# A two-layer encoder trunk: weight sums formed by adding transfers, seven products in the gate half of the second FFN, and the first output group moved forward

## The chip, the core and the metric

The kernel runs on one core of one Trainium2 chip. The time is the device time of one execution in microseconds, taken as the median of several executions. Before the change it was 1288.16 us, the median of three runs (1286.86 to 1289.29).

## The reference, cut to what matters

The trunk has two layers over 512 tokens of 1024 features. A layer mixes tokens (HGRN2 and stick-breaking heads in layer 0, an mLSTM in layer 1) and then runs a causal convolution FFN with a gate. The change is in the two FFNs ("the first network" and "the second network" below), each with an input projection of 1024 to 2 x 2816 and an output projection of 2816 to 1024.

```python
def conv_glu_ffn(h, w_in, conv_w, conv_b, w_out):
    u = jnp.matmul(h, w_in)
    a, g = jnp.split(u, 2, axis=-1)
    a = causal_dwconv(a, conv_w, conv_b)
    return jnp.matmul(jax.nn.gelu(a) * g, w_out)

x = x + g_f * conv_glu_ffn(modulate(x, norm_ffn_g, sh_f, sc_f), ffn_w_in, ffn_conv_w, ffn_conv_b, ffn_w_out)
```

The modulation vectors (`sh_f`, `g_f` and others) come from `c` through `ada_w`: 96 columns, each one transfer of 512 KB and one multiply-and-reduce on VectorE.

## The kernel before, in words

Everything is float32. Features lie on the 128 partitions, tokens along the row. Every operand of a large product is split into a high part (a cast to fp32r on ScalarE, L222) and a low part (the difference on VectorE, L223), and every product is three matmuls: high x high, high x low, low x high. `split_w` does this for weights, `split_act` for activations.

**An FFN (`ffn`, L1130).** The 22 column tiles of 128 of the `a` half and of the gate half are taken in pairs. Pairs 0 and 2 (the opening, the loop over `f0`) are computed directly. The nine pairs from 4 to 20 are "sets". In a set, the `a` half (2 tiles, 1024 x 256 weights against 1024 x 512 activations) is computed by the seven products of Strassen's scheme in its Winograd form (`Seven`): the weight is a 2 x 2 matrix of blocks (128 columns by 512 rows, 256 KB each), the activations too (512 features by 256 tokens). One product (X1 to X7, `Seven.run`) is 12 matmuls of 256 columns. The gate half is computed directly: Y0 and Y1 are 24 matmuls of 512 columns each (`second`).

The sums that the scheme needs are formed on VectorE. On the weight side, `Seven.fetch` loads the four blocks in two transfers, `Seven.prep` forms four sums into the `sums` tiles (L1083, L1084, L1087, L1088) and splits them. On the activation side, `tokens_side(kk)` forms and splits four sums for each of four feature tiles, once per FFN; two are formed after each tile of the second opening pair. `Seven.run` reads the partial results from the PSUM banks (copies `pp`, `u2` on ScalarE, additions into `v` on VectorE, L1113 to L1128). At the end of a set, `post` does the convolution (`act_a`), the activation, the gate and the split (`act_g`), and calls `take(2)`: two ada columns (only the first network has any left; `side`).

**The job list.** The products and gate tiles of a set are jobs, in `ORDER` (`FIRST` in set 4). Output projections (`out_jobs`) are jobs too: one per 256 output columns, with an x update (L385) per 128. Output columns are accumulated in groups of input tiles: six tiles, then four, four, four, and the last four by `halves_out` behind the list. Groups 0, 1 and 2 stand in the sets 6, 10 and 14 behind their third job, group 3 behind the last set. The loop at the end of `ffn` runs nine jobs ahead with the loads of the blocks (`FETCH`) and six ahead with the splits (`LEAD`). A planner orders the instructions of each engine from this program order by its own cost estimates, and places the semaphore waits.

**Queues and buffers.** All transfers are issued by SyncE, in order; one waits there until the buffer it writes is free. `raw` has four buffers of 4 KB per partition (weights as loaded), `sums` two, `ada` two, `ws` ten (split weights), `wq` two of half the size; `work` has 45 tiles for activations. PSUM has four banks `acc` and four `mx`. GpSimd issues no transfer and has small operations outside the FFNs.

## Time and profile before

| | |
|---|---|
| median of three runs | 1288.16 us |
| the profiled execution | 1288.47 us |
| its span | 1286.7 us |
| granted TensorE clock, mean | 0.995 |
| the first FFN, sets and output | about 351 to 645 us |
| the second FFN, sets and output | about 964 to 1253 us |

The page gives busy times for the whole span, then costly groups of instructions. Views of the trace give stretches of time, waits and single instructions. A group's line holds the line of the kernel, the engine, the operation, "out<-in" by tile names, the shape and the count, then busy time and the mean duration of one. TensorE's matmuls overlap, so what one costs is read from start to start.

### The profile page before, as it was taken

To read this page: it belongs to the slowest core of one execution; us is meant where nothing else is said; L and a number is where in the kernel's file an instruction comes from. 1 tells how busy PE (TensorE), PEld (TensorE's weight loads), DVE (VectorE), ACT (ScalarE), POOL (GpSimd) and SP (SyncE) were. 2 spreads that over 40 slices of the span, in tenths; PEclk is the share of its full clock that TensorE was granted. 3 is DMA by queue.
4 is the path that set the end of the run, shared out by engine and by line. 5 is a ranking of instruction groups with operands and counts; after the bars stand their busy time and mean duration, and the time that the engine had idled before them with its cause. 6 is when DMAs were issued, how large, how long until landed. Compare 5 with 4: busy or idle time off the path is not lost.

```text
span 1286.7 us, 18103 instructions
## 1 busy us (share of the span) xinstructions
PE 1246.4 (97%) x6942; PEld 1060.2 (82%) x6942; DVE 917.6 (71%) x1503; ACT 578.9 (45%) x1011; POOL 113.7 (9%) x199
## 2 busy tenths in 40 slices
PE   5999999999989999999999999999999999999997
PEld 4876788899878888888897777778988888888887
DVE  7845788857876776768776869776797475657665
ACT  4454323235452434344446674774455152525432
POOL 0021254400000000000000120221000000000000
PEclk9999999999999999999999999999999999999999
DMA  8823655422434343435423338522232332323211
GB/s 319 296 70 99 220 171 178 135 83 67 147 99 148 120 141 118 140 119 181 136 80 115 98 100 267 157 66 67 66 115 75 106 114 83 112 85 111 86 49 66
DMA packets 47078, 161.04 MB, mean 125 GB/s; under 512 B 5136, under 2 KB 7568, under 8 KB 46992
## 3 DMA queue, kind: packets, MB, share of 16 engines
q1 hardware_dynamic: 46992, 159.89, 38.8%
q8 instruction: 54, 0.88, 0.3%
q14 instruction: 32, 0.26, 0.1%
HBM read 157.77 MB, written 2.10 MB: 124 GB/s over the span
## 4 chain that ended last, share of the span: by engine, by line
PE 86%; DVE 5%; issue 3%; ACT 3%; DMA 2%; POOL 1%; SPq 0%; POOLq 0%; DVEq 0%; ACTq 0%
PE acc L255 13%; PE acc L256 13%; PE acc L257 13%; PE mx L255 5%; PE mx L256 5%; PE mx L257 5%; PE acc L1107 4%; PE acc L1108 4%; PE acc L1109 4%; PE acc L657 2%; PE mx L488 2%; PE mx L659 2%; PE acc L289 1%; PE acc L291 1%; PE acc L290 1%
## 5 line engine op out<-in xcount | busy, mean ns | idle before, releaser
L255 PE MATMUL acc<-hh,wg 128*128 128x512 f32 (+1 forms) x384 | 144.0, 376 | 1.2 <-DVE cv L1148 1.2
L256 PE MATMUL acc<-hl,wg 128*128 128x512 f32 (+1 forms) x384 | 144.4, 376 | 0.0
L257 PE MATMUL acc<-hh,wg 128*128 128x512 f32 (+1 forms) x384 | 144.1, 376 | 0.0
L169 DVE CUSTOM_DVE_ANT_0 adaraw<-adaraw,csb,par 128x1024 f32<-128x1024 f32 x96 | 123.0, 1293 | 4.3 <-DMA adaraw<-adaT 4.2
L256 PE MATMUL mx<-actl,wd 128*128 128x512 f32 x288 | 113.5, 394 | 0.0
L255 PE MATMUL mx<-acth,wd 128*128 128x512 f32 x288 | 112.8, 395 | 0.0
L257 PE MATMUL mx<-acth,wd 128*128 128x512 f32 x288 | 112.1, 394 | 0.0
L255 PE MATMUL acc<-hh,w 128*128 128x512 f32 x256 | 105.6, 412 | 0.0
L222 ACT CAST w<-wraw 128x1024 fp32r<-128x1024 f32 x68 | 71.2, 1051 | 68.5 <-PE acc L256 35.0
L257 PE MATMUL acc<-hh,w 128*128 128x512 f32 x256 | 101.9, 398 | 0.0
L256 PE MATMUL acc<-hl,w 128*128 128x512 f32 x256 | 101.7, 397 | 0.0
L223 DVE TENSOR_TENSOR w<-wraw,w 128x1024 fp32r<-128x1024 f32 x68 | 83.5, 1234 | 24.3 <-ACT w L222 14.6
L1107 PE MATMUL acc<-th,wa 128*128 128x256 f32 x288 | 83.3, 289 | 4.9 <-ACT th L1187 3.5
L222 ACT CAST wg<-wgraw 128x1024 fp32r<-128x1024 f32 x44 | 46.1, 1048 | 86.5 <-PE acc L1108 64.6
L385 DVE SCALAR_TENSOR_TENSOR x<-mx,mod,x 128x512 f32<-128x512 f32 x64 | 47.8, 749 | 52.1 <-PE mx L257 51.7
L255 PEld LDWEIGHTS acc<-hh,wg 128*128 128x128 f32 x384 | 72.1, 188 | 14.8 <-ACT wa L222 1.4
L257 PEld LDWEIGHTS acc<-hh,wg 128*128 128x128 f32 x384 | 72.0, 188 | 13.7 <-DVE wg L223 0.4
L1108 PE MATMUL acc<-tl,wa 128*128 128x256 f32 x288 | 81.7, 284 | 1.1 <-DVE tl L1188 1.1
L256 PEld LDWEIGHTS acc<-hl,wg 128*128 128x128 f32 x384 | 72.1, 188 | 12.3
L1109 PE MATMUL acc<-th,wa 128*128 128x256 f32 x288 | 81.4, 283 | 0.0
L336 POOL TENSOR_TENSOR nr<-nv,mhalf 128x2 f32<-128x2 f32 (+1 forms) x9 | 7.7, 854 | 815.4 <-ACT nv L334 815.4
L222 ACT CAST wa<-was 128x1024 fp32r<-128x1024 f32 x36 | 37.8, 1050 | 69.1 <-PE mx L256 29.8
(307 smaller groups left out, 3254.9 us busy)
## 6 DMA issues: line engine op xcount, KB each, us to landing
adaraw<-adaT SPq DMA_DIRECT2D x96, 512.0 KB, 4.4
wraw<-wflat SPq DMA_DIRECT2D x76, 512.0 KB, 4.2
waraw<-wflat SPq DMA_DIRECT2D x44, 512.0 KB, 3.7
wgraw<-wflat SPq DMA_DIRECT2D x44, 512.0 KB, 4.4
wdraw<-wflat SPq DMA_DIRECT2D x32, 512.0 KB, 3.8
x<-xT SPq DMA_DIRECT2D x8, 256.0 KB, 4.6
wdraw<-wflat SPq DMA_DIRECT2D x8, 256.0 KB, 2.7
outT<-fin SPq DMA_DIRECT2D x6, 256.0 KB, 2.4
```

Of the source, the lines that this page charges most:

```text
L169: return nc.vector.tensor_tensor_reduce(out=tile_, in0=tile_, in1=csb, scale=1.0, scalar=pc("ada_b", o), op0=ALU.mult, op1=ALU.add, accum_ ...
L222: nc.scalar.copy(hi, src)
L223: nc.vector.tensor_sub(lo, src, hi.bitcast(F32))
L255: nc.tensor.matmul(out, ah, bh, start=start, stop=False)
L256: nc.tensor.matmul(out, ah, bl, start=False, stop=False)
L257: nc.tensor.matmul(out, al, bh, start=False, stop=stop)
L385: nc.vector.scalar_tensor_tensor(x[j][:, sl], ps, g, x[j][:, sl], op0=ALU.mult, op1=ALU.add)
L488: nc.tensor.matmul(lps[:, c * 64:(c + 1) * 64].rearrange("p (b m) -> p b m", m=m), k[:, s], qu, start=True, stop=True)
L657: nc.tensor.matmul(vps[i], act[:, i * P:(i + 1) * P], wt_[:, 0:512], start=s0, stop=s1)
L1107: nc.tensor.matmul(ps, hi[:, ks], bh, start=first and kk == 0, stop=False, skip_group_check=True)
L1108: nc.tensor.matmul(ps, hi[:, ks], bl, start=False, stop=False, skip_group_check=True)
L1109: nc.tensor.matmul(ps, lo[:, ks], bh, start=False, stop=kk == 3, skip_group_check=True)
```

## The change

The weight sums are no longer formed on VectorE. The blocks of a half lie one after the other in HBM, and a sum is formed by loading one block pair into a tile and adding others onto it with transfers that accumulate (`accum_op`), which GpSimd issues. A seven-product half now takes seven tile pieces: for products 1 and 2 a plain load of two blocks; for 5 and 7 a load and one addition of two blocks; for 3 and 6 a load, two additions of two blocks and one of one block; for 4 a load of one. Each of the four steps is issued three jobs (`STAGE`) after the one before, the last three jobs before `LEAD` (5). The signs are taken over by the token side and by the evacuations (a factor -1 in an instruction that was there).

In the second network (`PAIRS`) the gate half goes through seven products as well, so a set there has 14 jobs (`TWO`). The output groups are four, four, four, four, two and four tiles, and stand in the sets 4, 8, 12 and 16, behind the third job (fourth in `TWO`); the group of two, with 512 columns per job, stands behind the last set. All token sums are formed at the first job instead of within the opening. The ada columns come one with each half of an output job (of 128 columns) of the groups after the first. `raw` now has two buffers inside the lists; two more each for the tiles `pr` and `qw`, and two halves `rawq`. Outside the lists weights take turns in `raw`, `pr` and `qw`. `work` has 44 tiles.

```diff
-    NW, NR, NS, NQ, NX, NA = 45, 4, 10, 2, 2, 2
+    NW, NR, NS, NQ, NA = 44, 2, 10, 2, 2
...
+    def load_blocks(tile_, at, i0, n, add=False):
+        o, m = at + i0 * P * T, n * P * T
+        eng = nc.gpsimd if add else nc.sync
+        eng.dma_start(tile_.rearrange("p (b c) -> p b c", b=n),
+                      wflat[o:o + m].rearrange("(b p c) -> p b c", b=n, p=P),
+                      **({"accum_op": ALU.add} if add else {}))
...
+    homes = ("raw", "pr", "qw")
+    turn = [0, 3]
+    def raw_tile(name, n=D, tag=None):
+        if n <= T:
+            return rawp.tile([P, T], F32, tag="rawq", name=nm(name), bufs=NQ)[:, :n]
+        if tag is None:
+            tag = homes[turn[0] % turn[1]]
+            turn[0] += 1
+        return rawp.tile([P, D], F32, tag=tag, name=nm(name))[:, :n]
...
-    ORDER = ("X1", "X5", "X6", "X2", "X7", "Y0", "X3", "X4", "Y1")
-    FIRST = ("Y0", "X1", "Y1", "X5", "X6", "X2", "X7", "X3", "X4")
-    PREPS = ("X1", "X5", "Y0", "X7", "X4")
-    OUT_AT, LEAD, FETCH = 3, 6, 9
+    ONE = ("X1", "X5", "X6", "X2", "X7", "Y0", "X3", "X4", "Y1")
+    ONE_FIRST = ("X1", "X2", "Y0", "X5", "X6", "Y1", "X7", "X3", "X4")
+    TWO = ("X1", "Y1", "X2", "Y2", "X5", "Y5", "X6", "Y6", "X3", "X7", "Y7", "Y3", "X4", "Y4")
+    LEAD, STAGE = 5, 3
+    PAIRS = (False, True)
...
+        def stages(self):
...
+            return {
+                1: [lambda: start(1, 0, 2)],
+                5: [lambda: add(5, 2), lambda: start(5, 1, 2)],
+                6: [lambda: load_blocks(t[6][:, 0:T], self.at, 3, 1, True), lambda: add(6, 2), lambda: add(6, 1),
+                    lambda: start(6, 0, 2)],
+                4: [lambda: start(4, 3, 1)],
+            }
         def prep(self, n):
-            (a11, a12), (a21, a22) = ((r[:, 0:T], r[:, T:D]) for r in self.raw)
...
-                nc.vector.tensor_add(src[:, 0:T], a21, a22)
-                nc.vector.tensor_sub(self.s2, src[:, 0:T], a11)
...
+            hi, lo = split_w(self.t[n], self.name)
+            for i, m in enumerate({1: (2, 1), 5: (7, 5), 6: (3, 6), 4: (4,)}[n]):
                 self.pieces[m] = hi[:, i * T:(i + 1) * T], lo[:, i * T:(i + 1) * T]
...
-        groups = ((0, 6), (6, 4), (10, 4), (14, 4), (18, 4))
+        groups = ((0, 4), (4, 4), (8, 4), (12, 4), (16, 2), (18, 4))
...
-                    tokens_side(2 * s)
-                    tokens_side(2 * s + 1)
-            take(2)
...
         def out_jobs(gi):
             f0, fn = groups[gi]
-            for cb in range(4):
+            cols = 1024 // fn
+            for cb in range(D // cols):
...
+                        if gi > 0:
+                            take(1)
...
+        def seven_at(sev, n, j):
+            for i, f in enumerate(sev.stages_of[n]):
+                fetches.append((j - LEAD - (i + 1) * STAGE, len(fetches), f))
+            return lambda: sev.prep(n)
...
             def post():
-                take(2)
                 for s in range(2):
-                    act_g(act_a(fi + s, first.v[s]), st[s])
+                    act_g(act_a(fi + s, sevens["X"].v[s]), sevens["Y"].v[s] if two else st[s])
...
-            set_jobs(fi, {6: 0, 10: 1, 14: 2}.get(fi))
-        out_jobs(3)
+            set_jobs(fi, {4: 0, 8: 1, 12: 2, 16: 3}.get(fi))
+        out_jobs(4)
+        fetches.sort(key=lambda e: e[:2])
...
+        for j, (_, run, post) in enumerate(jobs):
+            advance(j)
+            if j == 0:
+                for kk in range(4):
+                    tokens_side(kk)
             run()
```

## Rows read from the trace of the kernel before

**Rows 1.** The page, busy us, share of the span and instructions of each engine.

```profile
PE 1246.4 (97%) x6942; PEld 1060.2 (82%) x6942; DVE 917.6 (71%) x1503; ACT 578.9 (45%) x1011; POOL 113.7 (9%) x199
```

**Rows 2.** Stretches: start:end, length, busy us of engines (instructions), clock, DMA share, GB/s.

```profile
0.00:30.00 30.00, 17.02 (x62) 14.02 (x63) 21.44 (x37) 14.27 (x21) 3.17 (x11) 1.00 0.89 320
...
351.00:377.40 26.40, 20.90 (x134) 19.03 (x133) 22.30 (x37) 13.58 (x21) 0.00 (x0) 0.94 0.35 103
366.00:369.30 3.30, 2.98 (x15) 2.99 (x16) 3.30 (x7) 0.71 (x4) 0.00 (x0) 0.59 0.15 14
412.30:640.00 227.70, 227.70 (x1287) 196.61 (x1286) 164.71 (x226) 95.30 (x135) 0.00 (x0) 1.00 0.42 139
971.00:985.00 14.00, 12.28 (x94) 11.38 (x93) 11.26 (x18) 7.81 (x13) 0.00 (x0) 1.00 0.35 111
1182.20:1203.40 21.20, 21.20 (x134) 18.99 (x133) 15.34 (x22) 10.55 (x17) 0.00 (x0) 1.00 0.32 100
```

**Rows 3.** Waits of TensorE, whole span: for whom, us in total, times, longest.

```profile
PE acc L1107 <- ACT th L1187: 3.5, 1, 3.5
...
PE acc L255 <- DVE cv L1148: 1.2, 1, 1.2
...
PE acc L1108 <- DVE tl L1188: 1.1, 2, 0.8
...
PE acc L1107 <- DVE v L1124: 0.8, 2, 0.4
PE acc L1107 <- ACT pp L1113: 0.5, 1, 0.5
```

**Rows 4.** Timeline, second FFN: start us, duration us, instruction.

```profile
1023.34 0.39 PE L255 MATMUL acc<-hh,wg 128*128 128x512 f32 x1
...
1028.91 0.28 PE L1107 MATMUL acc<-hh,wa 128*128 128x256 f32 x1
...
1030.32 0.28 PE L1107 MATMUL acc<-th,wa 128*128 128x256 f32 x1
...
1031.73 0.39 PE L255 MATMUL acc<-hh,wg 128*128 128x512 f32 x1
...
1230.34 0.39 PE L255 MATMUL mx<-acth,wd 128*128 128x512 f32 x1
...
1234.51 0.69 DVE L251 TENSOR_TENSOR actl<-cv,acth 128x512 fp32r<-128x512 f32 x1
```

**Rows 5.** Groups of instructions, shapes apart, whole span; L1180 from 936 to 985 us.

```profile
L169 DVE CUSTOM_DVE_ANT_0 adaraw<-adaraw,csb,par 128x1024 f32<-128x1024 f32 x96 | 123.0, 1293 | 4.3 <-DMA adaraw<-adaT 4.2
...
L385 DVE SCALAR_TENSOR_TENSOR x<-mx,mod,x 128x512 f32<-128x512 f32 x64 | 47.8, 749 | 52.1 <-PE mx L257 51.7
...
L223 DVE TENSOR_TENSOR wa<-was,wa 128x1024 fp32r<-128x1024 f32 x36 | 44.0, 1223 | 21.1 <-ACT wa L222 20.5
...
L222 ACT CAST wa<-was 128x1024 fp32r<-128x1024 f32 x36 | 37.8, 1050 | 69.1 <-PE mx L256 29.8 <-PE acc L256 23.6 <-PE acc L1108 12.1
...
L1083 DVE TENSOR_TENSOR was<-waraw 128x512 f32<-128x512 f32 x18 | 12.4, 686 | 3.2 <-DMA waraw<-wflat 3.1
...
L1121 DVE TENSOR_TENSOR v<-mx,pp 128x256 f32<-128x256 f32 x18 | 7.5, 418 | 1.3 <-PE acc L1109 1.2
...
L1113 ACT COPY pp<-acc 128x256 f32<-128x256 f32 x18 | 6.6, 367 | 0.9 <-DVE actl L251 0.8 <-PE acc L256 0.2
...
L1180 DVE SCALAR_TENSOR_TENSOR tu<-hraw,mod,tu 128x256 f32<-128x256 f32 x4 | 1.9, 478 | 0.0
```

**Rows 6.** The page, DMA issues: tile, count, size, us from issue to landing.

```profile
adaraw<-adaT SPq DMA_DIRECT2D x96, 512.0 KB, 4.4
...
waraw<-wflat SPq DMA_DIRECT2D x44, 512.0 KB, 3.7
...
wdraw<-wflat SPq DMA_DIRECT2D x8, 256.0 KB, 2.7
```

**Rows 7.** Waits of SyncE's queue, whole span: us in total, times, longest.

```profile
SPq L200 <- DVE wa L223: 173.9, 37, 17.1
```

More of the change, by code (lines that the diff above doesn't have):

```diff
@@ L241, in load_split @@
             k1 = min(k0 + ku, kn)
[L242 removed]
+            raw = raw_tile(name + "raw", (k1 - k0) * cols)
             load(raw, [(wname, i, r0 + k0 * P, r0 + k1 * P, c0, c1)])
@@ L1232, in run @@
                             mm3(ps, *st["w"].get(k, sl), *acts[f0 + k], k == 0, k == fn - 1)
-                        x_update(ps, layer, 1, cb * 2 + s)
-                jobs.append((None, prep, run, None))
-        def set_jobs(fi, outs):
-            first = Seven(w, fi * P, bs, "wa")
+                        x_update(ps, layer, 1, cb * (cols // P) + s)
+                        if gi > 0:
+                            take(1)
+                jobs.append((prep, run, None))
+        def seven_at(sev, n, j):
+            for i, f in enumerate(sev.stages_of[n]):
+                fetches.append((j - LEAD - (i + 1) * STAGE, len(fetches), f))
+            return lambda: sev.prep(n)
+        def set_jobs(fi, outs):
+            two = pairs
+            sevens = {"X": Seven(w, fi * P, bs, "wa")}
+            if two:
+                sevens["Y"] = Seven(w, F + fi * P, bs, "wg")
+            for sev in sevens.values():
+                sev.stages_of = sev.stages()
             st = {}
@@ L1248, in post @@
             def post():
-                take(2)
                 for s in range(2):
-                    act_g(act_a(fi + s, first.v[s]), st[s])
-            order = FIRST if fi == 4 else ORDER
+                    act_g(act_a(fi + s, sevens["X"].v[s]), sevens["Y"].v[s] if two else st[s])
+            order = TWO if two else ONE_FIRST if fi == 4 else ONE
+            out_at = 4 if two else 3
+            base = len(jobs)
+            pos = {name: i for i, name in enumerate(order)}
             for i, name in enumerate(order):
-                if i == OUT_AT and outs is not None:
+                if i == out_at and outs is not None:
@@ L1256, in set_jobs @@
                     out_jobs(outs)
                 n = int(name[1])
-                p = PREPS[i] if i < len(PREPS) else None
                 prep = None
-                if p:
-                    prep = second_prep if p[0] == "Y" else lambda n=int(p[1]): first.prep(n)
-                jobs.append((first.fetch if i == 0 else None, prep,
-                             (lambda n=n: first.run(n)) if name[0] == "X" else lambda n=n: second(n),
-                             post if i == len(order) - 1 else None))
@@ L1266, in ffn @@
-        for fi in range(4, NF, 2):
-            set_jobs(fi, {6: 0, 10: 1, 14: 2}.get(fi))
-        out_jobs(3)
-        nf = npr = 0
-        for j, (_, _, run, post) in enumerate(jobs):
-            while nf < min(j + FETCH, len(jobs)):
-                if jobs[nf][0]:
-                    jobs[nf][0]()
-                nf += 1
+                if name[0] in sevens:
+                    sev = sevens[name[0]]
+                    if n in (1, 5, 6, 4):
+                        prep = seven_at(sev, n, len(jobs))
+                    run = lambda sev=sev, n=n: sev.run(n)
+                else:
+                    if n == 0:
+                        prep = second_prep
+                    run = lambda n=n: second(n)
@@ L1275, in ffn, with advance @@
+                jobs.append((prep, run, post if i == len(order) - 1 else None))
+        for fi in range(4, NF, 2):
+            set_jobs(fi, {4: 0, 8: 1, 12: 2, 16: 3}.get(fi))
+        out_jobs(4)
+        fetches.sort(key=lambda e: e[:2])
+        npr = 0
+        def advance(j):
+            nonlocal npr
+            while fetches and fetches[0][0] <= j:
+                fetches.pop(0)[2]()
             while npr < min(j + LEAD, len(jobs)):
-                if jobs[npr][1]:
-                    jobs[npr][1]()
+                if jobs[npr][0]:
+                    jobs[npr][0]()
```

96 lines of the change are left out of this document (48 added, 48 removed).

## The prediction, made before the result was known

> **What bounds the kernel now.** I read the page's busy times first: TensorE is busy for 97% of the span, VectorE for 71%, ScalarE for 45%, GpSimd for 9% [rows 1]. A busy TensorE may still be a waiting one, so I went on to the table by stretches [rows 2]. From 412.3 to 640.0 us (sets of the first FFN) and from 1182.2 to 1203.4 us (one set of the second) TensorE is busy for every microsecond at clock 1.00. There only columns count: the time falls only if TensorE gets fewer of them, and work taken off VectorE gives nothing back by itself. The two exceptions are the starts of the job lists, 351.0 to 377.4 and 971.0 to 985.0, where TensorE lacks 5.5 and 1.7 us. The waits of TensorE name the releasers: copies and differences of the token sums, `th`, `tl`, a late `cv` and evacuations [rows 3]; all of them sum to 7.1 us. After the longest of them the granted clock of 366.0 to 369.3 is 0.59 [rows 2], a mixture of the 2.4 GHz level and the 1.2 GHz level; the 3.3 us did 0.59 of their work, which lost another 3.3 x 0.41 = 1.4 us.
>
> **The change part by part.**
>
> *Gate half of the second network as seven products.* The unit prices are read off start times [rows 4]: one 512-column gate tile runs from 1023.34 to 1028.91, 5.57 us for 24 matmuls; one product runs from 1028.91 to 1030.32 and the next to 1031.73, 1.41 us each for 12 matmuls of 256 columns. So a 256-column matmul costs 0.1175 us and a 512-column one 0.232, and narrow matmuls lose only 1%. A set is now 7 x 1.41 + 2 x 5.57 = 21.0 us and becomes 14 x 1.41 = 19.7 us: 1.27 us less, in 9 sets **-11.4 us**, all on the path that sets the end.
>
> *What feeds it.* VectorE in a set without output jobs is busy 15.3 of 21.2 us [rows 2]. From it go four sums of 0.685 and two splits of 1.22 [rows 5], 5.2 us; to it come three and a half splits (3 x 1.22 + 0.685) and three evacuations of 0.42, 5.6 us. That leaves 15.7 of 19.7 us, 80%. ScalarE, busy 10.6 of 21.2 us, loses two casts of 1.05 and gets three and a half (3.8 us) and four copies of 0.37: 13.8 of 19.7 us. Both fit, but they work in order, and the copy of one product must be done before a product two to three places later adds to the same bank. I count nothing for that by itself; where it turns into a wait, it is behind a late transfer, below.
>
> *Sums by adding transfers.* Per seven-product half, 4 blocks of 256 KB are loaded now. Afterwards it is 7 plain blocks and 7 that are added to what lies in SBUF, issued by GpSimd, which does nothing in these stretches [rows 2]. No row shows an adding transfer. The nearest rows are plain ones: 3.7 us from issue to landing for 512 KB and 2.7 us for 256 KB [rows 6]. Below, an addition costs as a plain one; above, it costs two passes, 7.4 and 5.4 us. The longest chain is that of X6: a start, two additions of 512 KB, one of 256 KB, each waiting for the one before. It takes 3.7 + 2 x 3.7 + 2.7 = 13.8 us at the low end and 3.7 + 2 x 7.4 + 5.4 = 23.9 at the high end. Its start is issued 17 jobs ahead of its product, its split 4 ahead. In the tightest place, set 20 behind set 18, those are 13 products, 18.3 us, to the split and 3.3 more to the product. The middle price, 18.9 us, is 0.6 us late at the split and in time for TensorE; the high end is 2.3 us late for it. Volume is the other limit. A set without output jobs takes 28 blocks, 7.34 MB in 19.7 us, 372 GB/s, and with the set that has them (22.3 us of output, 2.1 MB) it is 16.8 MB in 61.8 us, 271 GB/s. The opening 30 us moved 320 GB/s at a share of 0.89 [rows 2], 360 at full share, so at the plain price it goes with little to spare. I take a price near the plain one, as the only kind of transfer the trace has, and allow 1 us of late landing for each of the five sets without output jobs: **+5 us**, bounds 0 and +60 (worked out under the second rival). In the first network seven products were there before; 2.74 us of sums per set go from VectorE where TensorE did not wait for them: 0. Its chains have 9 jobs of 21 us per set to land in: 0, up to +6 if a set waits 0.7 us.
>
> *Buffers.* Plain weight tiles have two slots under the name `raw` inside the job list instead of four; an output or gate tile needs 3.7 us to land and 2.3 to be split, and one is wanted each 5.57 us, so two slots do. SyncE's loads stand in one queue; its load line waited up to 17.1 us for a slot before [rows 7] and TensorE did not notice, because jobs are prepared ahead (six then, five now). Outside the lists weights have six slots: 0, since no wait of TensorE there is for a weight.
>
> *First output group in the first set.* The token sums (per k one difference of 0.42 us, three of 0.48 and two of 0.69 [rows 5], 3.2 us, 13 in all) come behind the two pairs of the opening instead of between their matmuls. What covers them is X1, X2, Y0 (X1, Y1, X2, Y2 in the second network) and four output jobs, 8.4 or 5.6 + 22.3 us, before the first product that reads them. So the waits of rows 3 and the slow clock, 8.5 us, should mostly go. If VectorE's queue holds the sums behind x updates and splits, none does: 0 to -8.5, I take **-6 us**. Output columns are the same in number; eight more x updates per network, 8 x 0.75 us, lie under matmuls. At the end 2 output jobs (11.1 us) instead of 4 cover the last activations, which ended 4.9 us after the last gate tile, from 1230.34 to 1235.2 [rows 4]: 0. If that cover went too, up to 4.9 us would show.
>
> *Moved ada columns.* 24 transfers of 512 KB and 24 reductions of 1.29 us [rows 5] came two per set, behind its last job; now one comes with each half output job of the groups after the first. There VectorE has 8 x 1.29 + 8 x 0.75 + 4 x 1.22 = 21.2 of 22.3 us, besides the convolution and gating of the set before. The transfers stand in SyncE's queue among the output weights. Four banks give the x updates about 8 us of delay: 0, at most 4.4 us (one transfer's landing [rows 6]) for each of three groups, +13.
>
> Sum: the profiled execution took 1288.5 us (span 1286.7 and 1.8 around it), 0.3 above the median of the three runs. 1288.5 - 11.4 - 6.0 + 5.0 = 1276.1, and against the median **1276 us**.
>
> **Rivals.** *Late landings in sets without output jobs.* If ScalarE's cast waits for a sum, the evacuations behind it wait too. For: 80% of VectorE, and between 351.0 and 377.4, where VectorE was busy 22.3 of 26.4 us, TensorE stood. Against: from 412.3 to 640.0 it was busy for 72%, and TensorE waited for nothing [rows 2]. Price: 2.3 us (the high end above) in each of five sets, 11.5 in place of 5: 1283.
>
> *Adding takes two passes, and the transfers bound the second FFN.* This ends on the other side. An addition that reads its destination too occupies the transfer engines twice. A half is then 7 + 14 = 21 blocks, 5.5 MB, nine sets with output weights 108.5 MB. At 360 GB/s that takes 301 us, at the 320 that were seen 339, against 9 x 19.7 + 89 + 11 = 278 us of TensorE. The excess of 23 to 61 us takes the place of the 5: 1288.2 - 17.4 + 23 to 61 = 1294 to 1332, middle 1313. It decides from about 1.65 passes on (278 us carry 97 MB at 350 GB/s). Starts that wait for a slot then hold SyncE's queue, and output weights behind them. Against: the share is only 0.32 to 0.42 in the FFNs now [rows 2]. The Trainium skill ("Collectives: The Full Stack", in Part 3 on the fold count) says that a reducing transfer reads two sources and so runs at half the rate of a copy, 1.93 times as long in its measurement. No run here shows it; by that rule this rival would be the outcome.
>
> *The first network gives the gain back.* The ada columns crowd VectorE beside the output groups: +13 as above, and nothing is gained in the first sets: 1288.2 - 11.4 + 5 + 13 = 1295 at worst, 1288 with half of it, which I take. For: VectorE is full there for 22.3 us at a time. Against: the jobs on both sides leave it idle for more than a quarter.
>
> **How the numbers follow.** The forecast has 0.52, late landings 0.13, two passes 0.25, the first network 0.10. Three runs of this kernel lie within 0.2% (2.6 us) of each other, so I count 1285.6 to 1290.8 as no change. Faster: 0.51 + 0.11 = 0.62; same 0.01 + 0.02 + 0.07 = 0.10; slower 0.25 + 0.03 = 0.28. The range begins at 1267, below the sum with all first-set waits gone and no new ones (1268), and reaches to the middle of the second rival, 1313. The forecast alone has 1268 to 1284.
>
> **What would show it.** Right: 14 products in 19.7 us in the second FFN, TensorE busy throughout, no wait for `th` in either first set, adding transfers landing in 4 to 5 us. Wrong: ScalarE casts or TensorE waiting for a transfer into `waraw` or `wgraw` in the sets without output jobs, a DMA share above 0.9 there, landings of 7 us and more, or a long queue on GpSimd. If the set lasts longer than 21.0 us, the second rival holds.

## The result and the profile after

The changed kernel takes 1366.2 us (median of 4 runs, 1362.7 to 1368.4) against 1288.2 us: 1.060 times as long, 95% interval 1.059 to 1.062. The prediction was 1276 us; its range ended at 1313. The profiled execution took 1364.2 us.

The page of the changed kernel (busy us, share of the span, instructions; the DMA share in 40 slices, tenths; queues with packets, MB, share of 16 engines) answers to [rows 1]:

```profile
PE 1258.8 (92%) x7266; PEld 1084.1 (80%) x7266; DVE 909.9 (67%) x1492; ACT 604.5 (44%) x1069; POOL 236.2 (17%) x307
...
DMA  8832755427489888865133474127679899999921
...
q1 hardware_dynamic: 64560, 181.13, 40.4%
q0 software_dynamic: 25920, 49.55, 21.9%
```

TensorE falls from 97% to 92% busy, and only the transfer engines come near to being full in its place: 9 tenths in the last slices of the second FFN. `q0` is GpSimd's queue; all its transfers add. A MB of it costs 21.9 / 49.55 = 0.442% of the span, a MB of SyncE's queue 40.4 / 181.13 = 0.223%: 1.98 times as much.

Stretches of the kernel before, columns as in [rows 2]: each FFN, from its first product to the first one of the last output group.

```profile
298.56:645.32 346.76, 341.21 (x1920) 294.73 (x1919) 254.16 (x367) 146.07 (x211) 0.70 (x1) 1.00 0.41 131
912.00:1252.53 340.53, 338.75 (x1921) 293.75 (x1920) 229.56 (x322) 144.11 (x210) 0.70 (x1) 1.00 0.30 93
```

The same two of the changed kernel, then all nine sets, the middle of them, and two sets from one first output job to the next; last a stand of TensorE (a stretch in which it has nothing it can start) and what follows the stand:

```profile
298.50:652.33 353.83, 343.88 (x1920) 296.22 (x1919) 240.23 (x343) 144.66 (x213) 41.62 (x37) 0.99 0.74 198
917.63:1328.35 410.72, 349.60 (x2244) 317.73 (x2243) 235.04 (x336) 169.31 (x264) 82.63 (x73) 0.93 0.80 188
966.10:1328.40 362.30, 302.63 (x1946) 275.74 (x1945) 202.85 (x283) 146.67 (x229) 73.69 (x65) 0.92 0.82 191
1022.25:1291.73 269.48, 224.02 (x1474) 206.02 (x1474) 143.17 (x190) 107.03 (x167) 63.67 (x56) 0.92 0.92 213
1053.87:1133.11 79.24, 66.79 (x435) 60.47 (x433) 42.30 (x56) 31.20 (x48) 18.20 (x16) 0.94 0.92 216
1095.00:1103.20 8.20, 0.01 (x1) 0.01 (x1) 0.55 (x1) 1.63 (x3) 1.20 (x1) 0.78 1.09 284
1103.20:1107.00 3.80, 3.80 (x20) 3.80 (x21) 2.63 (x4) 0.85 (x2) 1.26 (x2) 0.58 0.56 171
```

Most of the loss is in the second FFN: 340.5 to 410.7 us. The first FFN loses another 7.1 us, and all else together gains 1.4. Of the second FFN's 70 us, 59 are idle time of TensorE (410.72 - 349.60 = 61.1 against 1.8) and 11 are busy time, although its products are shorter (without any sums, in e_nosum below, it is 7.4 us less busy than before): the clock is 0.93 on average. One stand shows how that goes. First the largest wait of TensorE (answering [rows 3]), then the timelines of ScalarE and TensorE around the stand, then the four transfers of the chain that it waited for and the start of the next chain:

```profile
PE acc L1125 <- ACT wg L236: 47.8, 8, 10.1
```

```profile
1101.57 1.04 ACT L236 CAST wa<-waraw 128x1024 fp32r<-128x1024 f32 x1 [8.43 <-DMA waraw<-wflat]
1102.52 0.61 ACT L236 CAST wg<-wgraw 128x512 fp32r<-128x512 f32 x1
...
1103.19 0.58 PE L1125 MATMUL acc<-th,wg 128*128 128x256 f32 x1 [8.21 <-ACT wg L236]
...
1103.78 0.41 PE L1125 MATMUL acc<-hh,wa 128*128 128x256 f32 x1
1103.99 0.41 PE L1126 MATMUL acc<-hl,wa 128*128 128x256 f32 x1
...
1106.95 0.28 PE L1126 MATMUL acc<-tl,wg 128*128 128x256 f32 x1
1107.07 0.28 PE L1127 MATMUL acc<-th,wg 128*128 128x256 f32 x1
```

```profile
1073.38 0.37 SPq L206 DMA_DIRECT2D waraw<-wflat  x1
...
1081.10 1.20 POOL L206 DMA_DIRECT2D waraw<-wflat  x1 [8.09 <-DVE x L399]
1087.43 1.20 POOL L206 DMA_DIRECT2D waraw<-wflat  x1 [5.13 <-DMA waraw<-wflat]
...
1093.83 0.90 POOL L206 DMA_DIRECT2D waraw<-wflat  x1 [3.96 <-DMA waraw<-wflat]
...
1103.90 0.37 SPq L206 DMA_DIRECT2D waraw<-wflat  x1
```

TensorE names ScalarE, but ScalarE stood 8.43 us itself, at the cast of the next set's sum for product 6, whose chain of adding transfers had not landed. Behind it in ScalarE's order stood a short cast whose data was there, and that is the one TensorE needed. All the while the transfer engines were full (a share of 1.09 by the profile). The chain took 28.2 us from the issue of its start to the cast (1073.38 to 1101.57); in the trace the other chains of product 6, in the sets from 994 us on, take 28 to 36 us to their last landing. After the stand a matmul starts every 0.21 us (1103.78, 1103.99), later again every 0.12 (1106.95, 1107.07); the granted clock of the 3.8 us is 0.58, a mixture of 1.2 and 2.4 GHz. So by an estimate 8.2 us of stand cost about 1.6 us more (3.8 x 0.42).

Landings, to be set beside [rows 6]:

```profile
waraw<-wflat POOLq DMA_DIRECT2D x54, 512.0 KB, 7.2
wgraw<-wflat SPq DMA_DIRECT2D x53, 512.0 KB, 4.9
...
wgraw<-wflat POOLq DMA_DIRECT2D x27, 512.0 KB, 8.4
```

### The profile page after: what moved, and what is told of

The parts are those of the page before. It is cut to its first block, busy times and chain, and to the rows that moved or that the text cites. A ratio compares the mean times of both kernels' runs of the same rounds, so it can differ in the third digit from the quotient of the medians.

```text
span 1362.5 us, 19173 instructions
## 1 busy us (share of the span) xinstructions
PE 1258.8 (92%) x7266; PEld 1084.1 (80%) x7266; DVE 909.9 (67%) x1492; ACT 604.5 (44%) x1069; POOL 236.2 (17%) x307
## 3 DMA queue, kind: packets, MB, share of 16 engines
q1 hardware_dynamic: 64560, 181.13, 40.4%
q0 software_dynamic: 25920, 49.55, 21.9%
## 4 chain that ended last, share of the span: by engine, by line
PE 60%; DMA 17%; DVE 10%; issue 6%; ACT 4%; POOL 2%; SPq 0%; POOLq 0%; DVEq 0%; ACTq 0%
PE acc L269 9%; PE acc L271 9%; PE acc L270 9%; DMA waraw<-wflat 6%; DMA wdraw<-wflat 4%; DMA wgraw<-wflat 4%; PE acc L1125 3%; PE acc L1126 3%; PE acc L1127 3%; PE mx L269 3%; PE mx L270 2%; PE mx L271 2%; DMA adaraw<-adaT 2%; PE mx L502 2%; PE acc L671 1%
## 5 line engine op out<-in xcount | busy, mean ns | idle before, releaser
L206 POOL DMA_DIRECT2D waraw<-wflat x72 | 86.0, 1206 | 433.6 <-DMA waraw<-wflat 383.5
L236 ACT CAST wa<-waraw 128x1024 fp32r<-128x1024 f32 (+1 forms) x80 | 75.5, 949 | 133.5 <-DMA waraw<-wflat 44.5
L237 DVE TENSOR_TENSOR wa<-waraw,wa 128x1024 fp32r<-128x1024 f32 (+1 forms) x80 | 87.8, 1101 | 64.1 <-ACT wa L236 63.0
L269 PE MATMUL mx<-acth,wd 128*128 128x512 f32 x288 | 115.6, 405 | 4.7 <-ACT acth L264 3.5
L271 PE MATMUL mx<-acth,wd 128*128 128x512 f32 x288 | 115.1, 401 | 0.7 <-DVE wd L237 0.7
L236 ACT CAST wg<-wgraw 128x1024 fp32r<-128x1024 f32 (+1 forms) x62 | 61.2, 986 | 102.4 <-DMA wgraw<-wflat 53.1
L237 DVE TENSOR_TENSOR w<-wraw,w 128x1024 fp32r<-128x1024 f32 x68 | 83.2, 1231 | 23.9 <-ACT w L236 14.5
L269 PE MATMUL acc<-hh,wg 128*128 128x512 f32 (+1 forms) x240 | 88.2, 369 | 3.3 <-DVE cv L1174 2.0
L271 PE MATMUL acc<-hh,wg 128*128 128x512 f32 (+1 forms) x240 | 88.5, 370 | 2.6 <-DVE wg L237 2.6
L237 DVE TENSOR_TENSOR wg<-wgraw,wg 128x1024 fp32r<-128x1024 f32 (+1 forms) x62 | 71.0, 1145 | 29.6 <-ACT wg L236 27.7
L270 PE MATMUL acc<-hl,wg 128*128 128x512 f32 (+1 forms) x240 | 88.0, 367 | 0.0
L1125 PE MATMUL acc<-th,wg 128*128 128x256 f32 x144 | 43.5, 302 | 47.8 <-ACT wg L236 47.8
L399 DVE SCALAR_TENSOR_TENSOR x<-mx,mod,x 128x512 f32<-128x512 f32 x80 | 59.2, 748 | 40.5 <-PE mx L271 40.5
```

The costliest lines, as they stand in the source:

```text
L206: eng.dma_start(tile_.rearrange("p (b c) -> p b c", b=n), wflat[o:o + m].rearrange("(b p c) -> p b c", b=n, p=P), **({"accum_op": ALU.add} ...
L236: nc.scalar.copy(hi, src)
L237: nc.vector.tensor_sub(lo, src, hi.bitcast(F32))
L269: nc.tensor.matmul(out, ah, bh, start=start, stop=False)
L270: nc.tensor.matmul(out, ah, bl, start=False, stop=False)
L271: nc.tensor.matmul(out, al, bh, start=False, stop=stop)
```

## The experiments

Theory: an adding transfer occupies the transfer engines twice as long as a plain one, and their volume bounds the second FFN. Rivals: the latency of the chains (each step waits for the one before); ScalarE's queue order.

**e_plain** leaves the additions out of the transfers.

```diff
-                      **({"accum_op": ALU.add} if add else {}))
+                      )
```

> Leaves out the additions in the transfers: the same 189 + 189 blocks of 256 KB come in by the same engines, in the same chains with the same waits, but GpSimd's transfers overwrite instead of adding, so the weight sums are wrong. Theory (the price of adding): in the changed kernel's table of queues an adding transfer costs 0.442% of the span per MB (21.9% for 49.55 MB), a plain one 0.223% (40.4% for 181.13 MB), so the nine sets of the second network need 158 plain blocks (41.4 MB, 126 us of all 16 engines) and 126 adding ones (33.0 MB, 199 us), together 325 us in a stretch of which the products fill about 275: the transfers are the bound. Without adding the same bytes take 226 us and are hidden: GpSimd's queue falls to about 11% of the span, the stands of 8 to 10 us at the ScalarE cast of the gate half go, and the time is 1276 to 1290 us. Rival (the chain's latency: GpSimd's issue of 1.2 us and four transfers that each wait for the landing of the one before): nothing of that changes, the stands stay and the time is above 1330 us.

1298.0 us (1.008 times the kernel before, interval 1.007 to 1.010): 68 us go with the adding alone. Bytes and chains are the same, GpSimd's queue has half its share; the page, then the two FFNs:

```profile
q0 software_dynamic: 13824, 49.55, 11.6%
```

```profile
298.41:644.10 345.69, 339.98 (x1921) 293.99 (x1919) 240.76 (x343) 144.98 (x213) 25.48 (x37) 1.00 0.62 203
910.90:1263.31 352.41, 337.47 (x2244) 307.53 (x2243) 234.97 (x336) 168.82 (x264) 49.80 (x73) 0.99 0.65 219
```

So the price of adding is most of the loss. Which side of that price, the time on the engines or the latency of a step, this run does not tell, since it takes both away: in its trace the chains of product 6 take 18 to 24 us. And the expected 1276 to 1290 was missed: even at the plain price the change loses 10 us. 14.8 us of short waits of TensorE are left in the second FFN, some with a slow clock behind them.

**m_transfers** moves 512 KB transfers by themselves (x is stored as it came); the last batch mixes six adding and six plain ones:

```python
N = 12
...
kinds = ((nc.sync, False), (nc.gpsimd, False), (nc.gpsimd, True))
for eng, add in kinds:
    for _ in range(6):
        move(eng, big[:, 0, :], add)
    barrier()
for eng, add in kinds:
    for i in range(N):
        move(eng, big[:, i, :], add)
    barrier()
...
```

> All computation left out (x is stored as it came): 512 KB transfers by themselves on an otherwise idle chip. Chains of six into one tile, each waiting for the one before: plain by SyncE, plain by GpSimd, adding by GpSimd; then batches of twelve into twelve regions at once, of each kind; then a batch of six adding and six plain mixed. Theory (adding moves twice the bytes through the engines): a batch of twelve plain takes 12 x 1.6 us = 19 us by 3.04 us per MB, one of twelve adding 38 us. Rival (adding costs latency, not throughput: the reading back waits inside each transfer): the chains differ by 2 us or more per transfer, and the batches by less than a third.

GpSimd's queue on the page, then the timeline: the seven barriers and two issues of GpSimd:

```profile
q0 software_dynamic: 6048, 22.02, 47.1%
```

```profile
32.99 0.18 DVE L93 COPY big<-big 128x12 f32<-128x12 f32 x1 [19.32 <-DMA big<-wflat]
37.51 0.54 POOL L90 DMA_DIRECT2D big<-wflat  x1 [3.29 <-DMA big<-wflat]
56.33 0.18 DVE L93 COPY big<-big 128x12 f32<-128x12 f32 x1 [23.16 <-DMA big<-wflat]
62.23 0.87 POOL L90 DMA_DIRECT2D big<-wflat  x1 [4.52 <-DMA big<-wflat]
89.67 0.18 DVE L93 COPY big<-big 128x12 f32<-128x12 f32 x1 [33.16 <-DMA big<-wflat]
108.86 0.18 DVE L93 COPY big<-big 128x12 f32<-128x12 f32 x1 [19.02 <-DMA big<-wflat]
128.16 0.18 DVE L93 COPY big<-big 128x12 f32<-128x12 f32 x1 [19.12 <-DMA big<-wflat]
162.05 0.18 DVE L93 COPY big<-big 128x12 f32<-128x12 f32 x1 [33.70 <-DMA big<-wflat]
188.09 0.18 DVE L93 COPY big<-big 128x12 f32<-128x12 f32 x1 [25.86 <-DMA big<-wflat]
```

The waits in brackets are the parts. Chains of six: 19.3, 23.2 and 33.2 us, so 3.2 us per step plain by SyncE, 3.9 plain by GpSimd, 5.5 adding. Batches of twelve: 19.0, 19.1 and 33.7 us, 1.77 times (with one chain step taken off as the first landing, 28.2 against 15.2, 1.85 times). Six adding and six plain take 25.9, near the mean of the two (26.4). So the batch costs nearly twice as much, not quite the 38 us expected, and a step of a chain is dearer too. On the throughput this answers the prediction's second rival. The Trainium skill ("Collectives: The Full Stack", Part 3 on the fold count) has 1.93 for the reduce-scatter of a ring, whose transfers read two sources; this case's 1.77 to 1.98, for another kind of transfer, are near it. What the second half of the time is spent on no run shows. The size of the packets is not the reason: in the changed kernel adding transfers go in packets half as large as e_plain's (25920 against 13824 for the same bytes), but here they do not (at 2 KB the 24 adding transfers alone would be 6144 packets, and the whole queue has 6048), and the price is nearly the same.

**e_direct**, the gate half direct in both networks, adding kept for the first halves: `PAIRS = (False, False)`.

> The gate half of the second network as direct products again; sums by adding stay in both networks. Theory (price of adding, bytes bound): the nine sets need 131 plain blocks (104 us) and 63 adding ones (99 us), 203 us beside some 288 us of products, as in the first network, which lost little; no stands over 4 us, and 1283 to 1293 us, no difference to the kernel before that can be told or one of a few us. Rival (any chain of adding transfers is late, whatever else moves, and ScalarE's queue passes it on): half as many chains, half of the 74 us lost stays, 1310 to 1330 us.

1299.5 us (1.011, 1.008 to 1.014): between the two theories. FFNs of 351.9 and 347.3 us against 346.8 and 340.5. With half the chains most of the loss is gone, so it grows faster than the number of chains, as it would where a resource fills up; but adding costs something in the first network too (e_vec below, with the same products and no adding transfer, has 340.0 and 342.0 us).

**e_lead**, earlier issue, and **e_plain_lead**, the same on e_plain.

```diff
+        LEAD, STAGE = (8, 5) if pairs else (5, 3)
```

> The changed kernel with its sums still by adding transfers, but loads and casts of the second network's sets issued earlier: 8 jobs ahead instead of 5, and 5 jobs between the steps of a chain instead of 3 (a job of these sets is one product of 1.41 us, where before a job was 2.3 us on average). Theory (bytes bound: the nine sets ask for 325 us of the transfer engines beside 280 us of products): earlier issue moves no byte, the sets stay above 325 us, the whole at 1325 to 1360 us. Rival (lead too short in time: 3 jobs are 4.2 us, an adding transfer lands in 7.2 us): the stands at the gate half's cast go and the time falls to 1276 to 1300 us.

1362.0 us, second FFN 408.4 us. But the edit did not bring the chains forward, so it does not test the latency. The chain that answers to the one shown above starts 28.1 us before its cast, there 28.2:

```profile
1065.46 0.37 SPq L206 DMA_DIRECT2D waraw<-wflat  x1
...
1093.60 1.04 ACT L236 CAST wa<-waraw 128x1024 fp32r<-128x1024 f32 x1 [8.93 <-DMA waraw<-wflat]
...
1095.92 0.37 SPq L206 DMA_DIRECT2D waraw<-wflat  x1
```

The tile of these chains (`qw`) has two slots for two halves. In every second set the next start is issued 2.3 us after the cast of the set before, in both kernels (1101.57 to 1103.90, 1093.60 to 1095.92), about the time of that cast (1.04) and of VectorE's difference behind it (1.2): it waits for the slot, so a lead in jobs could not move it. More slots for the chains were not tried. What speaks for volume is the share: in the changed kernel the transfer engines are at 0.92 from 1022 to 1292 us, so steps without any latency could shorten that stretch by some 8% (an estimate, 22 us). How far full engines lengthen the chains and how far the chains keep the engines from being full the runs do not separate.

> As the kernel without additions in the transfers (its sums wrong as there: GpSimd's transfers overwrite), with the same longer leads as the run before this one. Without additions 14.8 us of waits stood in the second network, most of them at casts that waited for a late load, and some 13 us of slower clock and refilling behind them, which made it 352.4 us long against 340.5 us in the kernel before. Theory (the lead, counted in jobs, fell in time when the jobs became shorter): the waits fall below 5 us, the network to 333 to 342 us, the time to 1278 to 1288 us. Rival (the waits are ScalarE's and VectorE's own order and load at the end of a set): 350 us and 1295 to 1300 us as without the longer leads.

1311.1 us (1.018), second FFN 363.1: worse by 13 us than without the leads. Longer leads in jobs do not take the waits that e_plain has left. The starts of the chains are held by the same two slots, so whether an earlier issue would help is not shown.

**e_pairs4** tries ScalarE's queue order on the changed kernel, with a second pair of tiles for the short casts: `tag="wq", ..., bufs=4` for `bufs=NQ`, and `NW` 42 to make room.

> The changed kernel with two pairs of the 512-column tiles into which the casts for product 4 go, instead of one (the work tiles go from 44 to 42 to make room), so that the gate half's cast for product 4 no longer has to wait for the product 4 of the other half. Sums by adding transfers as before. Theory (bytes bound): TensorE waits for the same landings at another place, the time stays above 1345 us. Rival (the order in ScalarE's queue turns a late landing into the stands of 8 to 10 us): the six stands of together 47.8 us go and the time falls below 1325 us.

1371.1 us, second FFN 413.8. The stands move to other instructions of ScalarE (29.0 us at `ACT wa`, 7.8 at `ACT v`) and stay. The place of this cast in the queue decides where the time is lost, not whether.

**e_sum6**: sums of 6 and 3 by VectorE, of 5 and 7 by an adding transfer.

```diff
+            if n == 6:
+                t[6] = raw_tile(self.name + "s", D, "qw")
+                nc.vector.tensor_add(t[6][:, T:D], t[1][:, T:D], t[5][:, T:D])
+                nc.vector.tensor_add(t[6][:, 0:T], t[1][:, 0:T], t[6][:, T:D])
```

> Both networks: the weight sums of products 6 and 3 are formed by VectorE from the loaded blocks and the sums of 5 and 7 (two additions of 512 columns per half, 0.685 us each); only the sums of products 5 and 7 come by an adding transfer. The gate half stays as seven products in the second network. Theory (price of adding): the nine sets need 122 plain blocks (97 us) and 36 adding ones (57 us), 154 us beside some 275 us of products; VectorE goes from 15.7 to about 18.4 us of a set's 19.7. The stands go and the time is 1268 to 1284 us, faster than the kernel before. Rival (ScalarE's queue order: the gate half's last cast stands behind the cast of the next set's sum of product 6, and there is one pair of its tiles): the cast of sum 6 now waits for VectorE instead of the transfers, stands of 2 to 4 us stay per set and the time is 1290 to 1315 us.

1316.6 us (1.022), second FFN 368.7: missed by both, nearer the rival, at another engine. The second FFN, and a wait of VectorE there:

```profile
911.62:1280.27 368.65, 341.97 (x2245) 312.99 (x2244) 255.66 (x372) 169.57 (x264) 22.46 (x19) 0.96 0.45 120
```

```profile
DVE was L1113 <- DMA waraw<-wflat: 23.9, 7, 5.7
```

An addition that waits for its transfer now stands at the head of VectorE's queue, and TensorE waits 23.5 us for VectorE's splits behind it. The transfer engines are at 0.45 here. So full engines are not needed for a loss of this kind: a late landing at the head of a queue that works in order is enough, and the second FFN is 28 us longer than before.

**e_vec** and **e_vec2**: no adding transfers; the four sums of a half by VectorE, in place, gate half direct (e_vec: `PAIRS = (False, False)`) or as seven products in the second network (e_vec2).

```diff
-                5: [lambda: add(5, 2), lambda: start(5, 1, 2)],
-                6: [...],
+                5: [lambda: start(5, 2, 2)],
+                6: [],
...
+            if n == 5:
+                nc.vector.tensor_add(t[5][:, T:D], t[5][:, 0:T], t[5][:, T:D])
+                nc.vector.tensor_add(t[5][:, 0:T], t[1][:, T:D], t[5][:, 0:T])
+            if n == 6:
+                t[6] = t[1]
+                nc.vector.tensor_add(t[6][:, T:D], t[1][:, T:D], t[5][:, T:D])
+                nc.vector.tensor_add(t[6][:, 0:T], t[1][:, 0:T], t[6][:, T:D])
```

> No adding transfers: all four weight sums of a half by VectorE, in place in the loaded tiles (four additions of 512 columns, 0.685 us each), gate half direct in both networks; kept of the change: the first output group in the first set, the token sums, the order of the jobs. Tells what these are worth without the transfers. By the prediction's term they give 6 us of 1288: 1279 to 1285 us. Rival (they give about 1 us, as the first network's 345.7 us against 346.8 us suggests where the adding costs nothing): 1285 to 1291 us.

1282.5 us (0.996, 0.994 to 0.998), as the prediction's term of -6 us had it. The gain is in the first FFN, 346.8 to 340.0; the second, 342.0, does not gain:

```profile
298.72:638.67 339.95, 338.10 (x1921) 293.08 (x1919) 261.74 (x379) 145.93 (x213) 0.70 (x1) 1.00 0.45 144
903.97:1246.01 342.04, 339.45 (x1921) 294.22 (x1919) 234.50 (x329) 145.30 (x211) 0.70 (x1) 1.00 0.30 94
```

> No adding transfers: all four weight sums of a half by VectorE in place, as in the run with both gate halves direct, but with the gate half as seven products in the second network; leads of 5 and 3 jobs as in the changed kernel. Beside that run only the gate half's way differs, so the difference is what seven products for both halves are worth at plain bytes. By the prediction's term (21.0 to 19.7 us per set) the second network falls from 342 to 331 us and the time to 1271 us. Theory after the runs so far (in a set without output jobs 14 short products follow each other, ScalarE's and VectorE's work of the set's end stands before the next set's first casts, 15 to 24 us of waits and as much again in slow clock and refilling): 352 to 368 us in the second network, 1292 to 1308 us in all.

1287.5 us (0.999), second FFN 347.0: seven products for both halves are 5 us longer than the direct gate half, less bad than my theory of that moment, far from the 331 of the prediction's term:

```profile
903.72:1250.67 346.95, 336.04 (x2245) 307.39 (x2244) 275.07 (x407) 170.54 (x263) 1.05 (x1) 0.99 0.31 100
```

The timelines of a set without output jobs, VectorE (first and last of 27 instructions without a pause) and ScalarE:

```profile
1056.20 1.23 DVE L237 TENSOR_TENSOR wg<-wgraw,wg 128x1024 fp32r<-128x1024 f32 x1 [0.47 <-ACT wg L236]
...
1074.49 0.69 DVE L265 TENSOR_TENSOR actl<-cv,acth 128x512 fp32r<-128x512 f32 x1
...
1073.40 0.62 ACT L264 CAST acth<-cv 128x512 fp32r<-128x512 f32 x1 [1.11 <-DVE cv L1181]
1073.93 0.64 ACT L1138 COPY pp<-acc 128x256 f32<-128x256 f32 x2
```

VectorE works from 1056.2 to past 1075 us without a gap; a ScalarE cast waits for its `cv`, the copy of a product stands behind that cast, and TensorE waits 1.95 us for the copy. Four such waits make 7.7 us, three of them with a slow clock behind them.

**e_nosum**, e_vec2 with the four additions left out.

> e_vec2 without its weight sums: the blocks are loaded and split as there, VectorE's four additions per half are left out in both networks (the products then use single blocks, so the sums are wrong). VectorE falls from 275 us to about 225 of the second network's 347 us, nothing else changes. Theory (VectorE's load binds in the sets without output jobs, where it works almost without a pause): second network 327 to 337 us; the first network, where its waits were 2 us already, unchanged at 340 us; time 1268 to 1278 us. Rival (tiles and order): 344 us or more, 1284 us or more.

1269.4 us (0.986, 0.985 to 0.988). The two FFNs:

```profile
298.07:635.37 337.30, 337.26 (x1921) 293.05 (x1920) 240.53 (x343) 145.40 (x213) 0.70 (x1) 1.00 0.45 145
900.45:1232.90 332.45, 331.35 (x2244) 302.84 (x2243) 234.51 (x336) 169.46 (x264) 0.70 (x1) 1.00 0.33 104
```

The second FFN is 14.5 us shorter than in e_vec2, with 1 us of waits. So VectorE's additions are what held e_vec2 back. The shorter products do not come through in full, though: two sets, from the end of one set's output jobs to the end of the next ones, take 63.4 us, nearly all of it busy, where the prediction's 19.7 + 19.7 + 22.3 make 61.7:

```profile
1041.22:1104.66 63.44, 63.35 (x434) 58.03 (x433) 42.27 (x56) 31.30 (x49) 0.00 (x0) 1.00 0.38 117
```

**e_spread**, **e_order**, **e_order_spread** and **e_plain_order** came before that and asked whether something else held e_vec2 (or e_plain) back: the output jobs dealt out, two to a set; the seven products of one half before those of the other:

```diff
+                if two and (i == 7 or i == 0 and fi > 4):
+                    gi, cb = todo.pop(0)
+                    out_jobs(gi, [cb])
...
-    TWO = ("X1", "Y1", "X2", "Y2", "X5", "Y5", "X6", "Y6", "X3", "X7", "Y7", "Y3", "X4", "Y4")
+    TWO = ("X1", "X5", "X6", "X2", "X7", "X3", "X4", "Y1", "Y5", "Y6", "Y2", "Y7", "Y3", "Y4")
```

> As the run before this one, but the output jobs of the second network are dealt out evenly: one at the start of each set from the second on and one behind its seventh product (5.6 us each), in place of four at once in every second set; the last one at the end. The same products, casts and loads. Theory (the waits stand where a set begins without any other product to cover the casts): the cover of 5.6 us takes them away, second network 327 to 336 us, time 1267 to 1277 us, faster than both kernels. Rival (VectorE's load, some 280 of 330 us, is the bound wherever the jobs stand): 345 us or more in the second network and 1285 us or more.

> As the run with all sums by VectorE and seven products for both halves (e_vec2, 1287.5 us, second network 347.0 us), with the order of the 14 products of a set changed alone: first the seven of the one half, then the seven of the gate half, instead of the two halves in alternation. A pair of split tiles is then in use for three or four products instead of seven, so that at most three of the five pairs are held at once instead of six. Theory (casts wait for the release of split tiles by TensorE): the casts come earlier, second network 328 to 337 us, time 1268 to 1278 us. Rival (VectorE's load and order, 275 of 347 us, set it): 344 us or more, 1285 us or more.

> The changed kernel with transfers that overwrite instead of adding (sums wrong as in e_plain, 1298.0 us, second network 352.4 us), and the order of e_order in the second network. Theory (split tiles): of the 28 us that e_plain's second network stands above its products' 324 us at least half go, 330 to 340 us, time 1275 to 1287 us. Rival (ScalarE's and VectorE's own load): no change, 350 us and 1295 us or more.

> Order as in e_order, and the output jobs dealt out, one at the start of each set from the second on and one behind the seventh product. Theory (split tiles): here both the tiles and the cover of the set's end are there, second network 326 to 334 us, time 1265 to 1274 us. Rival (VectorE's load and order): as e_spread, 348 to 352 us and 1288 to 1293 us.

e_spread 1291.7 us (second FFN 350.4), e_order 1294.4 (355.0), e_plain_order 1317.4 (373.2), and with both edits on e_vec2 1299.8 (357.6). All four theories fell: holding a split tile for a shorter time did not help, and the orders only moved the waits. In e_spread new ones came at the splits of output weights (5.3 us at VectorE's part, 3.6 at ScalarE's).

**e_tiles11** and **e_nosum_tiles11** have half a pair of split tiles more: `NS` 11 for 10, `NW` 42 for 44, on e_vec2 and on e_nosum.

> e_vec2 with 11 split tiles of 1024 columns instead of 10, half a pair more (work tiles from 44 to 42 to make room). Theory (VectorE's load): no change beyond 2 us, 1285 to 1290 us. Rival (casts wait for the release of split tiles by TensorE): 5 us or more less, 1274 to 1282 us.

> Both edits: no weight sums (left out as in e_nosum) and 11 split tiles. Theory (VectorE's load): as e_nosum. Rival (tiles): some 5 us or more under e_nosum.

e_tiles11 takes 1295.6 us as a whole, because the stretches outside lost (first FFN 342.7 us, between the FFNs 274.0 instead of 265.3). Why is open: e_pairs4 has 42 work tiles too, and 266.9 us between its FFNs. The second FFN has 341.9 us against 347.0, so the rival has 5 us there. Without the sums (1284.5 us) it is 332.7 against 332.5: an eleventh tile gives nothing once VectorE is free.

**e_mix_lead**: sums of 5 and 7 by GpSimd, of 6 and 3 by VectorE, longer leads.

> No adding transfers, gate half as seven products in the second network, longer leads (8 and 5 jobs): the sums of products 5 and 7 by GpSimd, those of 6 and 3 by VectorE, in place. Theory (with plain bytes and the longer lead the shorter products come through): VectorE works about 255 of the second network's 335 us, products fill 324 us of it, time 1270 to 1282 us, faster than the kernel before. Rival (VectorE's and ScalarE's order: a sum in VectorE's queue stands in front of what TensorE waits for, as the sums of 6 and 3 did for 23.5 us in the run with those alone): 1290 to 1310 us.

1310.2 us (1.017), second FFN 367.0. GpSimd's additions are slow, and VectorE's instructions of the same time are slow too; a group of GpSimd and one of VectorE there:

```profile
L1113 POOL TENSOR_TENSOR wgraw<-wgraw,wgraw 128x512 f32<-128x512 f32 x9 | 16.2, 1796 | 36.0 <-DMA wgraw<-wflat 35.9
...
L237 DVE TENSOR_TENSOR wa<-waraw,wa 128x512 fp32r<-128x512 f32 x8 | 9.8, 1228 | 0.0
```

**e_best**: e_vec2 with the gate half as seven products only in the sets that have output jobs.

```diff
-            two = pairs
+            two = pairs and outs is not None
```

> e_vec (all weight sums by VectorE, no adding transfers, 1282.5 us, second network 342.0 us) with the gate half as seven products only in the four sets of the second network that have output jobs (22.4 us of products beside their 19.7 us), direct in the other five. Theory (VectorE's load binds only in the sets without output jobs, the others have room for four more additions): the four sets give 1.3 us each, second network 335 to 338 us, 1275 to 1279 us. Rival (the seven products of the gate half bring waits in any set): 342 us or more in the second network and 1282 us or more.

1274.9 us (0.990, 0.989 to 0.992), faster than both kernels, with nothing left out. The second FFN takes 335.0 us, 7.1 less than e_vec: TensorE is 4.9 us less busy (4 x 1.23, near the 1.27 per set of the prediction) and waits 2.2 us less. VectorE works 254 of it:

```profile
902.55:1237.51 334.96, 334.54 (x2065) 297.81 (x2064) 254.09 (x365) 157.41 (x235) 0.91 (x1) 1.00 0.31 100
```

## Why the prediction was wrong, step by step

**The price of an adding transfer** is the step that failed. The prediction took "a price near the plain one", +5 us. Measured it is 1.98 times the share of the engines per MB, 5.5 against 3.9 us per step of a chain alone, and 7.2 to 8.4 us to landing in the kernel. From e_nosum (same products, no sums anywhere) to the changed kernel it is 1366.2 - 1269.4 = 97 us: 68 for the adding (e_plain) and 29 for the bytes and chains at the plain price (231.9 MB on e_plain's page, 168.2 on e_nosum's). Of those 29 the runs do not say how much is volume and how much the chains. The reason given, that the trace has no other kind of transfer, was no reason: the upper bound of two passes was as near, and a rule for it was at hand. Nor was there room at the plain price: the prediction's own 372 GB/s for a set without output jobs is above its 360 at full share, which it read as "little to spare".

**The longest chain** was counted at 13.8 to 23.9 us. It took 28.2 us in the set shown and 28 to 36 in the others; at the plain price, in e_plain, 18 to 24. Its prices were landings in the kernel before, whose transfer engines are at 0.30 to 0.41 in the FFNs; here they are at 0.92 for most of the second.

**The second rival** is what happened in outline: adding costs about twice, and the transfer engines fill up. "If the set lasts longer than 21.0 us, the second rival holds" was the right test: two sets, one of them with output jobs, take 79.2 us where the sums have 61.7. But its 1313 us, and even its upper end of 1332, were too small, at two places. It let TensorE's work and the transfers run side by side, one full and the other hidden, with an excess of 23 to 61 us over TensorE's 278. By the shares per MB the nine sets need 325 us of transfers (41.4 MB x 3.04 us + 33.0 MB x 6.03 us, from the page after). They took 362 us from the start of the first set to the last output group (966.1 to 1328.4), an excess of 84, because the engines are not full all the time (a share of 0.82), and the stands slow TensorE behind them (a clock of 0.92). And it left the first FFN out: 353.8 us against e_nosum's 337.3, where 0 to +6 was counted.

**Seven products for the gate half, -11.4 us.** A single product of 12 matmuls takes 1.41 us in e_nosum too. But two sets take 63.4 us there and not 61.7, so 28 products cost 1.7 us more than 28 times the unit price; at a clock of 1.00 and with 0.1 us of waits neither of these explains it, and what does is open. The second FFN of e_nosum is 8.1 us shorter than before, so the term was 3.3 us too large even with every weight in time. In the four sets of e_best it held, 1.23 us each.

**VectorE and ScalarE, 0.** Right as counted: with that load TensorE waits 1 us (e_nosum). The 15.7 of 19.7 us leave 4.0 us in a set without output jobs; the eight additions of e_vec2 ask for 5.5 (8 x 0.685) and take 14.5 us of the gain back (347.0 against 332.5).

**Buffers, 0.** More split tiles gave nothing without VectorE's sums (e_nosum_tiles11), nor more tiles for the short casts with adding transfers (e_pairs4). The two slots of `raw`, and the two of `qw` that hold the starts of the chains, were not tried by themselves.

**First output group in the first set, -6 us.** Right in the first FFN, -6.8 us by e_vec, where the 3.5 us wait for `th` of [rows 3] is gone; but the second became 1.5 us longer in the same run, where the term had it shorter too.

**Moved ada columns, 0 to +13.** The runs show 0: e_vec has them, and its first FFN waits 1.8 us in all. The third rival falls with that.

Without any sums the change is worth 1288.2 - 1269.4 = 19 us, about the 17.4 of the two gains in the prediction. That the sums agree is partly luck: the first FFN gives 9.5 of it (346.8 to 337.3) and the second 8.1, where the prediction had its larger part in the second, and no kernel can leave the sums out. What the change did with the sums cost five times that.

## What to carry to other kernels

A transfer that adds is not a free addition: here it held the transfer engines 1.8 to 2 times as long as a plain one, so count every such byte twice before the sum of bytes is compared with the time. Where a price is not in the trace, and one bound of it turns the sign of the result, measure that price by itself (a few transfers suffice) before anything is built on the nearer bound. Count the work of an engine in the shortest stretch, not over the whole: in e_vec2 VectorE is busy for 275 of 347 us, but 15.7 + 5.5 us do not fit into a set of 19.7. Put extra work into the stretches that another engine's long work covers, as e_best does. And before a longer lead is taken as a test of latency, look in the trace whether the issue has moved.

## What was not expected of the hardware

- GpSimd's issue of an adding transfer takes longer than that of a plain one: 0.87 against 0.54 us by itself, 1.2 to 1.3 us in the loaded kernel (0.68 to 0.69 for the plain ones of e_plain).
- In e_mix_lead, where GpSimd adds, VectorE's eight splits of 512 columns for `wa` take 1228 ns on average, against 683 in e_vec, and GpSimd's own addition takes 1.36 to 1.80 us where VectorE takes 0.69.
- Twelve transfers that add take 33.7 us and twelve plain ones 19.0 (6.3 MB each), so the adding rate is about 187 GB/s against 331, first landing included.
